# Two-layer decoder trunk on one core: another order of the first two groups of three FFNs, an earlier transpose in the last group, and lower bounds computed on all partitions

## The chip, the cores and the metric

The kernel runs on one core of a Trainium2 chip. The metric is device time in microseconds (us) of one execution. Engines are named as in the profile: PE (matrix multiply; PEld is its weight load), DVE (vector), ACT (scalar), POOL (GpSimd), SP (which issues nearly all DMAs).

## The reference

Two layers, each a half-step SwiGLU FFN, a token mixer and a second half-step FFN, with a layer norm after each. `x` is 256 x 1024, the FFN's inner width is 2816, all in float32.

```python
def swiglu(x, w_gate, w_up, w_down):
    return (jax.nn.silu(x @ w_gate) * (x @ w_up)) @ w_down

lb_all = jnp.cumsum(jax.nn.softmax(lb_param.astype(f32), axis=0), axis=0)
lb_all = lb_all - lb_all[0:1]
for l in range(DEPTH):                                            # DEPTH = 2
    x = layer_norm(ALPHA * x + 0.5 * swiglu(x, ffn1_gate[l], ffn1_up[l], ffn1_down[l]), ln_g[l, 0], ln_b[l, 0])
    h = x @ w_in[l]
    u = h[..., :D_POOL]
    q, f_raw, v, g = jnp.split(h[..., D_POOL:], 4, axis=-1)
    y_pool = multiscale_pool(u, pool_w[l], pool_scale[l])
    o = hgrn2_recurrence(q, f_raw, v, lb_all[l])                  # uses log(lb) and log1p(-lb)
    y_hgrn = head_rms_norm(o, hgrn_norm_g[l]) * jax.nn.silu(g)
    mix = jnp.concatenate([y_pool, y_hgrn], axis=-1) @ w_out[l]
    x = layer_norm(ALPHA * x + mix, ln_g[l, 1], ln_b[l, 1])
    x = layer_norm(ALPHA * x + 0.5 * swiglu(x, ffn2_gate[l], ffn2_up[l], ffn2_down[l]), ln_g[l, 2], ln_b[l, 2])
```

`lb_param` is 2 x 512. In layer 0 the lower bound is zero, so its logarithms (`la` and `lm`) are read only in the mixer of layer 1.

## The kernel before

There are four FFNs; in the order of time they are called FFN1 to FFN4 here. FFN1 and FFN3 are followed by a mixer each, FFN2 by FFN3. The 256 tokens are two halves `hf` of 128 partitions.

**Split products.** Each float32 product is three PE matmuls (`mm3`, L95 to L97): weight and activation are each split into a rounded part and a remainder. Every 512 KB weight tile arrives by an SP DMA in `raw` (a ring of 5 buffers); ACT makes the rounded part (`wh`, `xh` or `dh`, L101), and behind it DVE the remainder (`wl`, `xl`, `dl`, L102). So each weight costs a turn of ACT and a turn of DVE in the order in which these stand in the engines' queues. The finished parts lie in three rings: `w` (8), `x` (2) and `d` (6).

**An FFN** works in 11 groups of 256 inner columns. `G(g, hf)` multiplies half `hf` by gate and up weights of group g (24 matmuls of 512 columns); `gate` (L335) then takes silu on ACT (`sil`, L340) and multiplies on DVE (`hn`, L341). `T(g, hf)` (L401) transposes `hn` on PE (L404, two matmuls) into a PSUM tile named `gu`; ACT and DVE copy it out as `hth` and `htl` (L101, L102). `D(g, hf)` multiplies that by the down weights (12 matmuls into `acc`). For the groups 2 to 9 `GT(g)` (L307) does both halves at once, already transposed. `D(10, hf)` is followed by the layer norm of that half, whose inverse square root is POOL's (`rs`, L253), and later by transposes of the result (L185) for the next stage.

**What sets the order.** PE's instructions stand in the order in which the program issues them. `later(n, fn)` puts a piece of work behind n further `mm3`; `T` is such a piece, with 6 slots, or 4 for the first half of group 0 and the second half of group 10. If something needs its result first, `later.wait` issues it at once. The other engines' instructions are placed by the framework's scheduler, by priorities: `AHEAD` moves the gate's and `T`'s pieces up, `BEHIND` puts the weight loads back. Each engine then works strictly through its list.

**PSUM.** All of `G`, `T` and `GT` draw their `gu` tiles in turn from a ring of 4. `GT` takes four at once, and its first four matmuls write one each; the fourth is the tile of whatever drew last before `GT`. Before `GT(2)` that is `T(1,1)`, and its tile is free when its `htl` is done.

**The order in an FFN (L434 to L469).** FFN2 to FFN4 run G(0,0) G(1,0) D(0,0) G(0,1) D(1,0) G(1,1) D(0,1) GT(2) D(1,1), then GT(g), D(g-1,0), D(g-1,1) for g from 3, and at the end G(10,0) D(9,0) D(10,0) G(10,1) D(8,1) D(9,1) D(10,1). FFN1 has an opening of its own.

**`lower_bounds` (L473)** works out `la` and `lm` near the end of FFN1. It takes the two rows of `lb_param` spread over 128 partitions (two DMAs of 256 KB into a `raw` tile), and every one of its 128 x 512 operations repeats one and the same row in all partitions.

Of the kernel before, what the change touches and what calls it, by code (L numbers as in the profile page):

```python
# [10 lines left out]
F32 = mybir.dt.float32  # L11
F32R = mybir.dt.float32r
U8 = mybir.dt.uint8
AF = mybir.ActivationFunctionType
# [3 lines left out]
P = 128  # L18
D = 1024
S = 256  # L20
DEPTH = 2
# [3 lines left out]
NG = DFF // GW  # L25
NB = 5
NH = 4
# [47 lines left out]
def trunk(ctx: ExitStack, tc: tile.TileContext, t, out: bass.AP):  # L75
    nc = tc.nc
    pool = lambda name, bufs, **kw: ctx.enter_context(tc.tile_pool(name=name, bufs=bufs, **kw))
    cp = pool("const", 1)
    rawp = pool("raw", RAW)
    wp = pool("w", NW)  # L80
    xp = pool("x", 3)
    xtp = pool("xt", 1)
    sp = pool("small", 2)
    gbp = pool("gb", 1)
    psa = pool("psa", 4, space=PSUM)
    psg = pool("psg", 4, space=PSUM)
    ctx.enter_context(tc.manual_schedule(engines={mybir.EngineType.PE}))
    later = Later()
# [101 lines left out]
    def project(hf, ps, ws):  # L190

        xt = xT[hf]
        for kt in range(KT):
            later.wait(lambda: xt.done > kt)
            wh, wl = ws[kt // 2].parts
            cs = slice((kt % 2) * 512, (kt % 2) * 512 + 512)
            mm3(ps, xt.h[:, kt, :], xt.l[:, kt, :], wh[:, cs], wl[:, cs], kt == 0, kt == KT - 1)
            if kt % 2:
                ws[kt // 2].used()
# [13 lines left out]
    fix = cp.tile([P, 4, PAD], F32, name="fix")  # L213
    pscale = cp.tile([P, DEPTH, 4], F32, name="pscale")
    gn = cp.tile([P, DEPTH], F32, name="gn")
    la = cp.tile([P, 512], F32, name="la")
    lm = cp.tile([P, 512], F32, name="lm")

    def late_dma(dst, src):

        tc.keep_in_program_order(nc.sync.dma_start(dst, src))

    def load_consts():
        for j in range(2):
            cm = rawp.tile([P, 1024], F32, name="raw")
            late_dma(cm, t["cumM"][:, j, :])
            nc.scalar.copy(cumM[:, j, :], cm)
        st = rawp.tile([P, 896], F32, name="raw")
        late_dma(st, t["masks"])
        nc.vector.tensor_copy(masks, st)  # L230
        late_dma(fix, t["fix"].to_broadcast([P, 4, PAD]))
        late_dma(pscale, t["pscale"])
        late_dma(gn, t["gn"])

    def load_gb(l, i):
        g = gbp.tile([P, D], F32, name="lng")
        b = gbp.tile([P, D], F32, name="lnb")
        late_dma(g, t["ln_g"][l, i:i + 1, :].to_broadcast([P, D]))
        late_dma(b, t["ln_b"][l, i:i + 1, :].to_broadcast([P, D]))
        return g, b  # L240
# [25 lines left out]
    class FFN:  # L266
# [17 lines left out]
        def G(self, g, hf):  # L284
            ps = psg.tile([P, 2 * GW], F32, name="gu")
            project(hf, ps, self.gw[g])
            self.gate(g, hf, ps)
# [48 lines left out]
        def gate(self, g, hf, ps):  # L336
            sil = scope[0].tile([P, GW], F32, name="sil", bufs=2)
            hn = scope[0].tile([P, GW], F32, name="hn", bufs=2)
            with tc.high_priority(offset=AHEAD):
                nc.scalar.activation(sil, ps[:, 0:GW], AF.Silu)  # L340
                nc.vector.tensor_tensor(hn, sil, ps[:, GW:2 * GW], ALU.mult)  # L341
            later(4 if (g, hf) in ((0, 0), (NG - 1, 1)) else 6, lambda: self.T(g, hf, hn))

        def start(self):

# [65 lines left out]
        def D(self, g, hf):  # L411
            if self.turned(g):
                ht = [[p[:, place[hf], :] for p in self.ht[g, i]] for i in range(2)]
            else:
                later.wait(lambda: (g, hf) in self.ht)
                ht = [[p[:, i, :] for p in self.ht[g, hf]] for i in range(2)]
            if g == 0:
                self.accs[hf] = [psa.tile([P, 512], F32, name="acc") for _ in range(2)]
            if g == 4 and hf == 0:
                self.gb = load_gb(*self.ln)  # L420
                if self.first:
                    load_consts()
                    for n in range(2):
                        load_x(n)
            dw = [w.parts for w in self.dw[g]]
            for c in range(2):
                cs = slice(c * 512, c * 512 + 512)
                for i in range(2):
                    mm3(self.accs[hf][c], ht[i][0], ht[i][1], dw[i][0][:, cs], dw[i][1][:, cs],
                        g == 0 and i == 0, g == NG - 1 and i == 1)  # L430
            for w in self.dw[g]:
                w.used()
            if g == NG - 1:
                layer_norm(hf, self.accs[hf], 0.5 / ALPHA, self.gb, self.slots[hf], self.last)  # L434

        def run(self):
            G, GT, D = self.G, self.GT, self.D
            if self.first:
                self.start()
                D(0, 0)  # L440
                D(0, 1)
                GT(2)
                D(1, 0)
                D(1, 1)
            else:
                G(0, 0)
                G(1, 0)
                D(0, 0)
                G(0, 1)
                D(1, 0)  # L450
                G(1, 1)
                D(0, 1)
                GT(2)
                D(1, 1)
            for g in range(3, NG - 1):
                GT(g)
                D(g - 1, 0)
                if g < NG - 2:
                    D(g - 1, 1)
            G(NG - 1, 0)  # L460
            D(NG - 2, 0)
            D(NG - 1, 0)
            G(NG - 1, 1)
            if self.mixer_next:
                tc.keep_in_program_order(nc.scalar.preload_act_table_set("natural_log_exp_and_others"))
            if self.first:
                with tc.high_priority(offset=-BEHIND):
                    lower_bounds()
            for g in range(NG - 3, NG):  # L469
                D(g, 1)  # L470


    def lower_bounds():  # L473

        pr = rawp.tile([P, 2, 512], F32, name="raw")
        for i in range(2):
            late_dma(pr[:, i, :], t["lb"][i:i + 1, :].to_broadcast([P, 512]))
        p0, p1 = pr[:, 0, :], pr[:, 1, :]
        m, r = la, lm
        nc.vector.tensor_tensor(m, p0, p1, ALU.max)  # L480
        for p in (p0, p1):
            nc.vector.tensor_tensor(p, p, m, ALU.subtract)
            tc.keep_in_program_order(nc.scalar.activation(p, p, AF.Exp))
        nc.vector.tensor_tensor(m, p0, p1, ALU.add)
        for c in range(4):
            cs = slice(c * P, (c + 1) * P)
            nc.vector.reciprocal(r[:, cs], m[:, cs])
        for p in (p0, p1):
            nc.vector.tensor_tensor(p, p, r, ALU.mult)
        nc.vector.tensor_tensor(p1, p0, p1, ALU.add)  # L490
        nc.vector.tensor_tensor(p1, p1, p0, ALU.subtract)
        nc.vector.tensor_scalar(p0, p1, -1.0, 1.0, ALU.mult, ALU.add)
        for dst, v in ((m, p1), (r, p0)):
            nc.vector.tensor_scalar_max(dst, v, TINY)
            nc.scalar.activation(dst, dst, AF.Ln)
            nc.vector.tensor_scalar(v, v, 0.0, NEG, ALU.is_le, ALU.mult)
            nc.vector.tensor_tensor(dst, dst, v, ALU.add)

    def log_sigmoid(dst, src, tmp):
        nc.scalar.activation(tmp, src, AF.Abs)  # L500
# [326 lines left out]
def _layout(inputs):  # L827
    a = {k: np.asarray(v) for k, v in inputs.items()}

    def gu(gate, up):  # L830
        both = np.stack([gate, up], axis=2).reshape(DEPTH, KT // 2, 2, P, 2, NG, GW)
        return both.transpose(0, 5, 1, 3, 2, 4, 6).reshape(DEPTH, NG, KT // 2, P, ET)

    w_in = a["w_in"].reshape(DEPTH, KT // 2, 2, P, NB, 512)[:, :, :, :, [2, 1, 3, 4, 0]]
    cum, masks, fix = _constants()
    return {
        "x": a["x"].reshape(S, D),
        "xT": a["x"].reshape(S, KT, P).transpose(2, 1, 0),
        "gu": np.stack([gu(a["ffn1_gate"], a["ffn1_up"]), gu(a["ffn2_gate"], a["ffn2_up"])], axis=1),
        "dn": np.stack([a["ffn1_down"], a["ffn2_down"]], axis=1).reshape(DEPTH, 2, DFF // P, P, D),  # L840
        "win": w_in.transpose(0, 4, 1, 3, 2, 5).reshape(DEPTH, NB, KT // 2, P, ET),
        "wout": a["w_out"].reshape(DEPTH, KT, P, D),
        "pw": a["pool_w"].transpose(0, 2, 1, 3),
        "pscale": a["pool_scale"].reshape(DEPTH, 4, P).transpose(2, 0, 1),
        "lb": a["lb_param"],
        "gn": a["hgrn_norm_g"].T,
        "ln_g": a["ln_g"],
        "ln_b": a["ln_b"],
        "cumM": cum,
        "masks": masks,  # L850
        "fix": fix,
    }
# [17 lines left out]
```

## Time and profile before

| | |
|---|---|
| median of 3 runs | 976.71 us (975.88 to 979.17) |
| profiled execution, its own time | 976.44 us |
| its span, first to last instruction | 974.7 us |
| ACT busy, DVE busy | 520.1 us (53%), 661.6 us (68%) |
| POOL busy | 26.2 us (3%) |
| mean DMA rate | 185 GB/s, 55% of the 16 DMA engines' time |
| granted PE clock, mean | 0.995 |
| the four FFNs' first GT(2) begins at | 35.98 (FFN1), 330.08 (FFN2), 520.15 (FFN3), 811.90 us (FFN4) |

Times within the span are counted from its first instruction. A row of the timeline has the start, the duration, engine, line, operation, what it writes and reads, and in brackets the idle time of the engine before it with what ended that. Matmuls overlap: a 512-column one is shown with 0.39 us, but the next starts 0.23 us after it. Waits on PE are therefore measured here from start to start.

### The profile page before, as it was taken

How to read it: one execution, taken by the hardware profiler on the slowest of the kernel's cores; microseconds unless marked ns; L12 is line 12 of the kernel's file. 1: busy time of each engine (PE TensorE's matmuls, PEld its weight loads, DVE VectorE, ACT ScalarE, POOL GpSimd, SP SyncE). 2: the span in 40 equal slices, each digit the busy share in tenths (PEclk: the TensorE clock that was granted, in tenths of full speed). 3: DMA queues.
4: the chain of work that ended last, by engine and by line, in shares of the span. 5: the costliest groups of instructions: out<-in, count | busy, mean ns of one | idle time of the engine just before them, and what ended most of it. 6: DMA issues, size and time to landing. Idle time of an engine off the chain costs nothing.

```text
span 974.7 us, 13133 instructions
## 1 busy us (share of the span) xinstructions
PE 957.0 (98%) x4814; PEld 808.3 (83%) x4814; DVE 661.6 (68%) x1095; ACT 520.1 (53%) x810; POOL 26.2 (3%) x47
## 2 busy tenths in 40 slices
PE   9999999999999899999999999999999999999996
PEld 7888888788887788888887888888888887888885
DVE  6875655899689675656675665547897896665625
ACT  6766544376555655554346555433965466645420
POOL 0000000000010000000000000000001000000000
PEclk9999999999999999999999999999999999999998
DMA  7977865233427866565346666542334377766301
GB/s 283 340 260 249 275 230 174 97 124 124 164 87 236 304 192 225 197 208 173 106 165 237 226 220 213 174 151 97 124 136 154 109 277 260 228 214 209 127 1 44
DMA packets 51473, 180.67 MB, mean 185 GB/s; under 512 B 6096, under 2 KB 6352, under 8 KB 51408
## 3 DMA queue, kind: packets, MB, share of 16 engines
q1 hardware_dynamic: 51408, 179.83, 55.0%
q8 instruction: 38, 0.62, 0.3%
q14 instruction: 27, 0.22, 0.1%
HBM read 178.75 MB, written 1.05 MB: 184 GB/s over the span
## 4 chain that ended last, share of the span: by engine, by line
PE 62%; DVE 4%; DMA 3%; ACT 1%; issue 1%; DVEq 0%; SPq 0%; ACTq 0%
PE gu L307 27%; PE acc L95 6%; PE acc L97 6%; PE acc L96 6%; PE gu L97 4%; PE gu L95 4%; PE gu L96 4%; DMA raw<-in_gu 2%; DVE wl L102 2%; DMA raw<-in_dn 1%; PE acc L652 1%; DVE dl L102 1%; PE gu L185 1%; ACT wh L101 0%; PE acc L624 0%
## 5 line engine op out<-in xcount | busy, mean ns | idle before, releaser
L101 ACT CAST wh<-raw 128x1024 fp32r<-128x1024 f32 (+1 forms) x204 | 209.9, 1035 | 101.9 <-DMA raw<-in_gu 46.1
L102 DVE TENSOR_TENSOR wl<-raw,wh 128x1024 fp32r<-128x1024 f32 (+1 forms) x204 | 241.6, 1200 | 24.9 <-ACT wh L101 14.2
L307 PE MATMUL gu<-xt,wh 128*128 128x512 f32 x768 | 179.7, 390 | 0.0
L102 DVE TENSOR_TENSOR dl<-raw,dh 128x1024 fp32r<-128x1024 f32 x88 | 106.8, 1224 | 104.8 <-ACT dh L101 104.7
L307 PEld LDWEIGHTS gu<-xt,wh 128*128 128x128 f32 x768 | 144.4, 188 | 30.4
L101 ACT CAST dh<-raw 128x1024 fp32r<-128x1024 f32 x88 | 91.6, 1048 | 115.4 <-DMA raw<-in_dn 111.5
L95 PE MATMUL acc<-dh,hth 128*128 128x512 f32 x352 | 139.2, 395 | 1.8 <-ACT hth L101 1.8
L96 PE MATMUL acc<-dl,hth 128*128 128x512 f32 x352 | 137.7, 391 | 0.3 <-DVE dl L102 0.3
L97 PE MATMUL acc<-dh,htl 128*128 128x512 f32 x352 | 137.6, 391 | 0.0
L95 PE MATMUL gu<-wh,xt 128*128 128x512 f32 x336 | 135.2, 402 | 0.0
L97 PE MATMUL gu<-wh,xt 128*128 128x512 f32 x336 | 131.4, 391 | 0.0
L96 PE MATMUL gu<-wl,xt 128*128 128x512 f32 x336 | 131.0, 390 | 0.0
L307 PE MATMUL gu<-xt,wl 128*128 128x256 f32 x768 | 99.7, 283 | 0.0
L307 PEld LDWEIGHTS gu<-xt,wl 128*128 128x128 f32 x768 | 96.9, 191 | 2.0
L330 DVE TENSOR_TENSOR sil<-gu,sil 128x256 f32<-128x256 f32 x64 | 27.0, 422 | 86.1 <-ACT sil L329 86.1
L95 PEld LDWEIGHTS acc<-dh,hth 128*128 128x128 f32 x352 | 66.2, 188 | 14.8 <-ACT hth L101 2.8
L97 PEld LDWEIGHTS acc<-dh,htl 128*128 128x128 f32 x352 | 66.1, 188 | 14.4 <-DVE htl L102 0.6
L96 PEld LDWEIGHTS acc<-dl,hth 128*128 128x128 f32 x352 | 66.2, 188 | 13.2 <-DVE dl L102 1.1
L97 PEld LDWEIGHTS gu<-wh,xt 128*128 128x128 f32 x336 | 63.1, 188 | 13.5
L96 PEld LDWEIGHTS gu<-wl,xt 128*128 128x128 f32 x336 | 63.3, 188 | 12.2
L95 PEld LDWEIGHTS gu<-wh,xt 128*128 128x128 f32 x336 | 63.2, 188 | 12.1
L307 PE MATMUL gu<-xt,xh 128*128 128x512 f32 x256 | 64.9, 405 | 5.0 <-DVE htl L102 5.0
(156 smaller groups left out, 1039.4 us busy)
## 6 DMA issues: line engine op xcount, KB each, us to landing
raw<-in_gu SPq DMA_DIRECT2D x172, 512.0 KB, 4.4
raw<-in_dn SPq DMA_DIRECT2D x88, 512.0 KB, 4.5
raw<-in_win SPq DMA_DIRECT2D x40, 512.0 KB, 4.1
raw<-in_wout SPq DMA_DIRECT2D x16, 512.0 KB, 4.4
lng<-in_ln_g SPq DMA_DIRECT2D x6, 512.0 KB, 4.8
lnb<-in_ln_b SPq DMA_DIRECT2D x6, 512.0 KB, 5.9
raw<-in_gu SPq DMA_DIRECT2D x8, 256.0 KB, 5.8
raw<-in_cumM SPq DMA_DIRECT2D x2, 512.0 KB, 5.5
```

Source lines behind the costliest of these rows:

```text
L95: nc.tensor.matmul(ps, lh, wh, start=start, stop=False)
L96: nc.tensor.matmul(ps, lh, wl, start=False, stop=False)
L97: nc.tensor.matmul(ps, ll, wh, start=False, stop=stop)
L101: first = nc.scalar.copy(dst_h, src)
L102: return first, nc.vector.tensor_tensor(dst_l, src, dst_h.bitcast(F32), ALU.subtract)
L185: nc.tensor.transpose(pt[:, k - a, :], self.nat[:, k * P:(k + 1) * P], ident)
L307: nc.tensor.matmul(ps[i][part][:, 2 * S - w:], weight.parts[lo][:, c:c + P], x[:, 0:w], start=kt == 0 and not lo, stop=kt == KT - 1 and lo ...
L330: nc.vector.tensor_tensor(dst, p[:, 0:S], dst, ALU.add)
L652: nc.tensor.matmul(ps[B][0:rows, j, :], E[:, j, s0:s0 + rows], E[:, j, t0:t0 + ps[B].shape[2]], start=True, stop=True)
```

## The change

Three things are done.

1. In FFN2 to FFN4, `G(1, 1)` comes before `D(1, 0)`.
2. The slots of `T` change. T(10,0) gets 2 in place of 6, T(1,1) gets 4 in place of 6, T(0,0) gets 6 in place of 4; T(10,1) keeps 4. This holds for FFN1 too.
3. `lower_bounds` works on the 512 values as 128 partitions x 4 for each of the two rows (`pr` and `both`, 128 x 2 x 4), so it needs one small load (`lbs`, 4 KB, issued with the other constants) in place of two spread ones. Its two results are written to a DRAM tile `rows` by a DMA on POOL's queue, and two more DMAs on POOL's queue spread each row over the partitions of `la` and `lm`.

```diff
+    drp = pool("rows", 1, space=bass.MemoryType.DRAM)
+    lbs = cp.tile([P, 2, NH], F32, name="lbs")
...
         late_dma(gn, t["gn"])
+        late_dma(lbs, t["lb"])
...
-            later(4 if (g, hf) in ((0, 0), (NG - 1, 1)) else 6, lambda: self.T(g, hf, hn))
+
+            slots = {(NG - 1, 0): 2, (NG - 1, 1): 4, (1, 1): 4}
+            later(slots.get((g, hf), 6), lambda: self.T(g, hf, hn))
...
                 G(1, 0)
                 D(0, 0)
                 G(0, 1)
+                G(1, 1)
                 D(1, 0)
-                G(1, 1)
                 D(0, 1)
                 GT(2)
                 D(1, 1)
...
     def lower_bounds():
 
-        pr = rawp.tile([P, 2, 512], F32, name="raw")
-        for i in range(2):
-            late_dma(pr[:, i, :], t["lb"][i:i + 1, :].to_broadcast([P, 512]))
+        pr = sp.tile([P, 2, NH], F32, name="pr")
+        both = sp.tile([P, 2, NH], F32, name="both")
+        nc.vector.tensor_copy(pr, lbs)
         p0, p1 = pr[:, 0, :], pr[:, 1, :]
-        m, r = la, lm
+        m, r = both[:, 0, :], both[:, 1, :]
         nc.vector.tensor_tensor(m, p0, p1, ALU.max)
         for p in (p0, p1):
             nc.vector.tensor_tensor(p, p, m, ALU.subtract)
-            tc.keep_in_program_order(nc.scalar.activation(p, p, AF.Exp))
+        tc.keep_in_program_order(nc.scalar.activation(pr, pr, AF.Exp))
         nc.vector.tensor_tensor(m, p0, p1, ALU.add)
-        for c in range(4):
-            cs = slice(c * P, (c + 1) * P)
-            nc.vector.reciprocal(r[:, cs], m[:, cs])
+        nc.vector.reciprocal(r, m)
...
         for dst, v in ((m, p1), (r, p0)):
             nc.vector.tensor_scalar_max(dst, v, TINY)
-            nc.scalar.activation(dst, dst, AF.Ln)
             nc.vector.tensor_scalar(v, v, 0.0, NEG, ALU.is_le, ALU.mult)
+        nc.scalar.activation(both, both, AF.Ln)
+        for dst, v in ((m, p1), (r, p0)):
             nc.vector.tensor_tensor(dst, dst, v, ALU.add)
+        rows = drp.tile([2, P, NH], F32, name="rows")
+        nc.gpsimd.dma_start(rows.rearrange("i p c -> p i c"), both)
+        for i, dst in enumerate((la, lm)):
+            nc.gpsimd.dma_start(dst, rows[i:i + 1].rearrange("i p c -> i (p c)").to_broadcast([P, 512]))
...
-        "lb": a["lb_param"],
+        "lb": a["lb_param"].reshape(DEPTH, P, NH).transpose(1, 0, 2),
```

What the scheduler makes of it is seen in the engines' orders at three places. Line numbers of the changed kernel are 1 to 8 higher than those of before.

**DVE and ACT in FFN2, ahead of GT(2).** First DVE before. `hn_3207` is the gate of (1,1), `htl_3228` the copy of T(1,1); the `dl` are the two down weights of group 2, `wl_3190` and `wl_3202` the first weights of group 4.

```order
L102 TENSOR_TENSOR htl_3149<-gu_3145,hth_3148 128x256
L102 TENSOR_TENSOR wl_3166<-raw_3164,wh_3165 128x1024
L102 TENSOR_TENSOR dl_3172<-raw_3170,dh_3171 128x1024
L102 TENSOR_TENSOR dl_3178<-raw_3176,dh_3177 128x1024
L341 TENSOR_TENSOR hn_3207<-sil_3206,gu_3138 128x256
L102 TENSOR_TENSOR wl_3190<-raw_3188,wh_3189 128x1024
L102 TENSOR_TENSOR wl_3202<-raw_3200,wh_3201 128x1024
L102 TENSOR_TENSOR htl_3228<-gu_3224,hth_3227 128x256
```

DVE in the changed kernel, at the same place; `hn_3198` and `htl_3217` are those of (1,1), `wl_3181` and `wl_3193` the first weights of group 4.

```order
L103 TENSOR_TENSOR htl_3176<-gu_3172,hth_3175 128x256
L103 TENSOR_TENSOR wl_3150<-raw_3148,wh_3149 128x1024
L344 TENSOR_TENSOR hn_3198<-sil_3197,gu_3129 128x256
L103 TENSOR_TENSOR dl_3156<-raw_3154,dh_3155 128x1024
L103 TENSOR_TENSOR dl_3162<-raw_3160,dh_3161 128x1024
L103 TENSOR_TENSOR htl_3217<-gu_3213,hth_3216 128x256
L103 TENSOR_TENSOR wl_3181<-raw_3179,wh_3180 128x1024
L103 TENSOR_TENSOR wl_3193<-raw_3191,wh_3192 128x1024
```

The gate's `hn` has moved ahead of both `dl`, and the copy `htl` ahead of both `wl`. ACT before, at the same place:

```order
L101 CAST dh_3177<-raw_3176 128x1024
L340 ACTIVATE sil_3206<-gu_3138 128x256
L101 CAST wh_3189<-raw_3188 128x1024
L101 CAST wh_3201<-raw_3200 128x1024
L101 CAST hth_3227<-gu_3224 128x256
```

ACT in the changed kernel:

```order
L102 CAST wh_3149<-raw_3148 128x1024
L343 ACTIVATE sil_3197<-gu_3129 128x256
L102 CAST dh_3155<-raw_3154 128x1024
L102 CAST dh_3161<-raw_3160 128x1024
L102 CAST hth_3216<-gu_3213 128x256
L102 CAST wh_3180<-raw_3179 128x1024
L102 CAST wh_3192<-raw_3191 128x1024
```

The silu of (1,1) now stands ahead of both `dh`, and the copy `hth` ahead of both `wh` of group 4. FFN4 has the same two pieces.

**DVE in FFN3, ahead of GT(2),** in the changed kernel (`hn_4876` and `htl_4895` are those of (1,1); `wl_4816` and `wl_4828` belong to group 3, `wl_4859` and `wl_4871` to group 4):

```order
L103 TENSOR_TENSOR wl_4816<-raw_4814,wh_4815 128x1024
L103 TENSOR_TENSOR wl_4828<-raw_4826,wh_4827 128x1024
L103 TENSOR_TENSOR dl_4834<-raw_4832,dh_4833 128x1024
L103 TENSOR_TENSOR htl_4854<-gu_4850,hth_4853 128x256
L103 TENSOR_TENSOR dl_4840<-raw_4838,dh_4839 128x1024
L344 TENSOR_TENSOR hn_4876<-sil_4875,gu_4807 128x256
L103 TENSOR_TENSOR wl_4859<-raw_4857,wh_4858 128x1024
L103 TENSOR_TENSOR wl_4871<-raw_4869,wh_4870 128x1024
L103 TENSOR_TENSOR htl_4895<-gu_4891,hth_4894 128x256
```

Here the two `wl` of group 3 have come ahead of `dl`, but `htl` of (1,1) still stands behind both `wl` of group 4, as it did before.

**POOL at the end of FFN1.** Before, the two powers `rs` (the layer norm's halves 0 and 1) had only the mixer's clearing of `sum` tiles between them:

```order
L253 TENSOR_TENSOR rs<-rs,neghalf 128x1
L726 MEMSET sum_2607 128x4x16
L726 MEMSET sum_2608 128x4x16
L726 MEMSET sum_2609 128x3x16
L726 MEMSET sum_2610 128x2x16
L253 TENSOR_TENSOR rs<-rs,neghalf 128x1
```

In the changed kernel the three DMAs stand there too:

```order
L256 TENSOR_TENSOR rs<-rs,neghalf 128x1
L503 DMA rows<-both 128x2x4
L505 DMA la<-rows 128x512
L505 DMA lm<-rows 128x512
L734 MEMSET sum_2610 128x4x16
L734 MEMSET sum_2611 128x4x16
L734 MEMSET sum_2612 128x3x16
L734 MEMSET sum_2613 128x2x16
L256 TENSOR_TENSOR rs<-rs,neghalf 128x1
```

POOL's second `rs` now stands behind three DMAs, of which the second and third read what the first writes.

## The prediction

> **What bounds the kernel now.** I read the page first, then the waits of PE, then the timeline around each of them.
>
> ```profile
> PE 957.0 (98%) x4814; PEld 808.3 (83%) x4814; DVE 661.6 (68%) x1095; ACT 520.1 (53%) x810; POOL 26.2 (3%) x47
> ```
>
> PE is busy in 98% of the span, and the change removes no matmul. So the time can fall only by what PE waits, and by what it runs slowly after a wait. The waits by kind (us in total, times, longest):
>
> ```profile
> PE gu L307 <- DVE htl L102: 5.0, 3, 2.2
> PE acc L95 <- ACT hth L101: 1.8, 4, 0.5
> ```
>
> Three waits in GT for a copy `htl`, and four of a down product for a copy `hth`: FFN2 to FFN4 have one of the former each, all four FFNs one of the latter. These rows count the time after the modelled end of the matmul before. What PE loses I take from start to start, against 0.23 us for a 512-column matmul.
>
> The worst place is the start of GT(2) in FFN2:
>
> ```profile
> 328.95 0.39 PE L96 MATMUL acc<-dl,hth 128*128 128x512 f32 x1
> 329.18 0.39 PE L97 MATMUL acc<-dh,htl 128*128 128x512 f32 x1
> 329.89 0.44 PE L404 MATMUL gu<-ident,hn 128*128 128x128 f32 x2 [0.32 <-DVE hn L341]
> 330.08 0.95 PE L307 MATMUL gu<-xt,xh 128*128 128x512 f32 x3
> 333.22 0.97 PE L307 MATMUL gu<-xt,xh 128*128 128x512 f32 x3 [2.19 <-DVE htl L102]
> ```
>
> 328.95 to 329.18 shows the step of 0.23. T(1,1) comes 0.71 after the last matmul: 0.48 lost. Three matmuls of GT take 0.69 from 330.08, so the fourth could start at 330.77 and starts at 333.22: 2.45 lost. Behind it PE runs slowly:
>
> ```profile
> 333.00:337.00 4.00, 3.78 (x11) 3.02 (x12) 0.31 (x2) 1.99 (x2) 0.00 (x0) 0.67 0.77 303
> 334.02 4.05 PE L307 MATMUL gu<-xt,xh 128*128 128x512 f32 x10
> ```
>
> The first row is a stretch (busy time by engine, then the granted clock): 0.67 there, 1.00 elsewhere. Ten matmuls take 4.05 us, where 9 x 0.23 + 0.39 = 2.46 would do: 1.6 lost. So FFN2 loses 0.5 + 2.4 + 1.6 = 4.5 us here.
>
> By the Trainium skill, "TensorE: Matmul & The Clock Gate", Part 1: The HAM clock gate, PE's clock is halved after an idle window of about 3.4 us, in windows that run free of the kernel; the trace differs, since an idle time under 2.5 us was enough here. What that rule makes of the sum is under the rivals.
>
> FFN3 and FFN4 have the same stop without the slow clock:
>
> ```profile
> 520.15 0.94 PE L307 MATMUL gu<-xt,xh 128*128 128x512 f32 x3
> 522.48 0.51 PE L307 MATMUL gu<-xt,xh 128*128 128x512 f32 x1 [1.38 <-DVE htl L102]
> ```
>
> ```profile
> 811.23 0.39 PE L97 MATMUL acc<-dh,htl 128*128 128x512 f32 x1
> 811.71 0.44 PE L404 MATMUL gu<-ident,hn 128*128 128x128 f32 x2
> 811.90 0.94 PE L307 MATMUL gu<-xt,xh 128*128 128x512 f32 x3
> 814.31 0.50 PE L307 MATMUL gu<-xt,xh 128*128 128x512 f32 x1 [1.47 <-DVE htl L102]
> ```
>
> FFN3: 522.48 - 520.15 - 0.69 = 1.6. FFN4: 814.31 - 811.90 - 0.69 = 1.7, and T itself came 0.25 late: 2.0. The three starts together: **8.1 us**.
>
> **T(10,0) two slots behind its gate.** FFN1 and FFN3 as examples:
>
> ```profile
> 174.58 0.44 PE L404 MATMUL gu<-ident,hn 128*128 128x128 f32 x2 [0.16 <-DVE hn L341]
> 175.48 0.50 PE L95 MATMUL acc<-dh,hth 128*128 128x512 f32 x1 [0.46 <-ACT hth L101]
> ```
>
> ```profile
> 657.44 0.38 PE L404 MATMUL gu<-ident,hn 128*128 128x128 f32 x2
> 658.28 0.50 PE L95 MATMUL acc<-dh,hth 128*128 128x512 f32 x1 [0.46 <-ACT hth L101]
> ...
> 655.39 0.42 DVE L341 TENSOR_TENSOR hn<-sil,gu 128x256 f32<-128x256 f32 x1 [5.19 <-ACT sil L340]
> ```
>
> Six slots are never reached, since D(9,0) has four and D(10,0) then asks for T at once. From T to the next matmul pass 0.84 us, of which the two transposes need 0.14: 0.7 lost, with 0.1 for a slow second matmul 0.8. With 2 slots T stands six matmuls (1.4 us) earlier, at about 656.0 in FFN3. Its input `hn` is done at 655.81, so T does not wait, and six matmuls then cover the 0.84 us of the copy. I take 0.8 in FFN2, FFN3 and FFN4. In FFN1 `hn` was late as well:
>
> ```profile
> 172.18 0.69 DVE L480 TENSOR_TENSOR la<-raw 128x512 f32<-128x512 f32 x1 [5.16 <-DMA raw<-in_lb]
> 172.90 1.29 DVE L482 TENSOR_TENSOR raw<-raw,la 128x512 f32<-128x512 f32 x2
> 174.11 0.41 DVE L341 TENSOR_TENSOR hn<-sil,gu 128x256 f32<-128x256 f32 x1
> ```
>
> Three operations of the old lower bounds stood ahead of it, waiting for their DMA. In the order of the change these have gone far ahead, with 4 elements in place of 512; `hn` then ends at about 172.6 and T is due at 172.9. FFN1 saves 0.8 + 0.4 = 1.2. Together **3.6 us**, in bounds 0 and 3.6.
>
> **G(1,1) ahead of D(1,0), T(1,1) after 4 slots.** T(1,1) now stands between D(1,0) and D(0,1): D(0,1)'s twelve matmuls, 12 x 0.23 = 2.7 us, lie between it and GT(2). What this brings hangs on when `htl` can be done. DVE and ACT in FFN2 before:
>
> ```profile
> 325.24 1.23 DVE L102 TENSOR_TENSOR wl<-raw,wh 128x1024 fp32r<-128x1024 f32 x1
> 326.39 1.22 DVE L102 TENSOR_TENSOR dl<-raw,dh 128x1024 fp32r<-128x1024 f32 x1
> 328.28 1.23 DVE L102 TENSOR_TENSOR dl<-raw,dh 128x1024 fp32r<-128x1024 f32 x1 [0.67 <-ACT dh L101]
> 329.42 0.42 DVE L341 TENSOR_TENSOR hn<-sil,gu 128x256 f32<-128x256 f32 x1
> 330.35 2.49 DVE L102 TENSOR_TENSOR wl<-raw,wh 128x1024 fp32r<-128x1024 f32 x2 [0.51 <-ACT wh L101]
> 332.75 0.42 DVE L102 TENSOR_TENSOR htl<-gu,hth 128x256 fp32r<-128x256 f32 x1
> ```
>
> ```profile
> 327.19 1.05 ACT L101 CAST dh<-raw 128x1024 fp32r<-128x1024 f32 x1 [1.04 <-DMA raw<-in_dn]
> 328.15 0.38 ACT L340 ACTIVATE sil<-gu 128x256 f32<-128x256 f32 x1
> ```
>
> The silu stood behind `dh`, which waited for its DMA, and `htl` behind the two `wl`. In the new order silu and `hn` go ahead of both `dl`, and `htl` comes right behind these. The `dh` still waits for its DMA and ends at 328.24; the second `dl` then ends at 329.51, `htl` at 329.9. PE, without the 0.48 of lateness, would start its fourth matmul of GT(2) at 330.77 - 0.48 = 330.3. So `htl` is in time by 0.4 us. T(1,1) is due at 329.41 - 2.7 = 326.7; `hn`, behind the `wl` that ends at 326.47, is done at 326.9: 0.2 late, which the sum takes off. FFN2 saves 4.5 - 0.2 = 4.3, the slow clock with it. FFN4 has the same pieces of order: 2.0. In FFN3 `htl` stays behind both `wl`; those of group 3 now come earlier, and with them their `raw` buffers, but how much of this reaches `htl` no row says. The bounds are 0 and 1.6; I take 1.2, nearer the whole, since the lead of 2.7 is more than the 1.6 to be hidden. Together **7.5 us**.
>
> What PE does next is covered: GT(2) then reads weights of group 2, which DVE has finished before the rows above begin (their first `wl` is group 3's). G(1,1) uses the weights that G(1,0) had. T(0,0), now 6 slots behind its gate, has two `mm3` (1.4 us) left before D(0,0), against the 0.84 us of the copy; should ACT or DVE be full there, D(0,0) waits, which I bound by 0 and 1 us in each FFN and take at 0.
>
> **Lower bounds.** Some twenty DVE operations of 128 x 512 (0.69 us in the row at 172.18) become as many of 128 x 4. PE waited for none of them but `hn`, counted above, so the rest is worth 0. The two DMAs on SP give way to one small one. The three DMAs on POOL delay only POOL's second `rs`:
>
> ```profile
> L257 DVE SCALAR_TENSOR_TENSOR x<-x,rs,lnb x24: 742/746/753, 181.7 to 970.8; 128x512 f32<-128x512 f32 x24
> L252 DVE TENSOR_SCALAR rs<-mv x12: 146/153/155, 180.3 to 968.8; 128x1 f32<-128x1 f32 x12
> L253 POOL TENSOR_TENSOR rs<-rs,neghalf x12: 917/924/997, 180.6 to 969.1; 128x1 f32<-128x1 f32 x12
> ```
>
> ```profile
> 202.07 0.60 PE L185 MATMUL gu<-ident,x 128*128 128x128 f32 x4
> 188.01 0.42 DVE L102 TENSOR_TENSOR htl<-gu,hth 128x256 fp32r<-128x256 f32 x1
> raw<-in_lb SPq DMA_DIRECT2D x2, 256.0 KB, 4.1
> ```
>
> The new chain starts behind the `htl` that ends at 188.4: 13 small DVE operations at 0.15 (L252's) are 2.0 us, ACT's logarithm at most 0.4; `both` is ready by 190.9. PE wants the normalised half at 202.07, so `rs` must start by 202.07 - 0.75 - 0.92 - 0.2 = 200.2. That leaves POOL 9.3 us for one DMA to land (4.1 by the `in_lb` row, for far more bytes) and for issuing three; no row shows an issue on POOL, so 0 to 0.9 each, the length of its own power. 4.1 + 2.8 = 6.9: in time by 2.4, so 0.
>
> **The sum.** 3.6 + 7.5 = 11.1 us. The profiled execution took 976.44 us, 0.3 below the median of the runs; 976.44 - 11.1 = **965.3 us**, or 1.1% faster.
>
> **The rivals.**
>
> *DVE stays late.* The scheduler's order was made by its own times. Where a DMA lands later than in the rows above, `htl` still comes after PE; margins are 0.4 us in FFN2, unknown in FFN3. If half of the 8.1 us stays, the time is 976.44 - 3.6 - 4 = 968.8; if all of it, 972.8. For it speaks the queue of DMAs in that stretch (share 0.77 in the row at 333); against it that `htl` no longer waits behind group 4 in two of three FFNs. Chance 0.18.
>
> *The slow clock is not the stop's doing.* If the 3.4 us at low clock come anyway, 1.6 us return: 966.9. By the Trainium skill's rule named above, stops under 3.4 us cost no clock, which would be this case. Against it: it began right behind the longest stop, and nothing else in the trace shows it between start and end. Chance 0.05.
>
> *POOL holds the layer norm: slower.* If the three DMAs keep POOL beyond 200.2, PE stands at the transposes of 202.07. From 9.3 us on it costs PE as much as it is late; slower than before by 0.3% it is from 11.1 + 2.9 + 9.3 = 23.3 us on. At 8 us for each DMA (twice the `in_lb` row) POOL is free at 214.9: 14.7 late, with the slow clock 16.3, or 981.6 us. At 4.1 each it is 3.0 late, 968.3. Against it: only the first DMA must land before the others are issued. By the Trainium skill, "SBUF — State Buffer", SBUF: two separate sides, a DMA on POOL's queue can't write its descriptors while DVE runs a two-port operation, and one of 620 ns took 3100 so; three of that are 9.3 us, an estimate from that page, just at the limit. No run here shows such a DMA. Chance 0.06, of which 0.02 slower than before.
>
> *The change does nothing:* if other waits take all of it, 976. Chance 0.03.
>
> **How the numbers follow.** The forecast has 0.68, within 963 and 967. Low end: the sum with FFN3's whole 1.6 and T(1,1) not late is 11.7, and D(0,0) of FFN2, with the 1 us bounded above, could as well gain as lose it: 963.7, with some scatter 963. High end: to 970, which takes in half of the first rival, the clock, and POOL's 968.3. A measurement of this kernel tells 0.3% (2.9 us) from no change; so faster means under 973.5. Faster 0.93, same 0.05, slower 0.02.
>
> **What would show it.** In the changed profile: no GT wait for `htl` in PE's waits, or a small one in FFN3; no `acc` wait for `hth`; a granted clock of 1.00 between start and end; T(10,0) in the midst of D(9,0); POOL's second `rs` before 200; FFN1 shorter by 1.2. It would be wrong if PE waited at T(1,1) or T(10,0) instead, at D(0,0) for the later T(0,0), or at the transposes behind FFN1.

## The result, and the profile after

| | before | after |
|---|---|---|
| median | 976.71 us (5 runs, 974.63 to 979.17) | 968.14 us (5 runs, 967.02 to 968.72) |
| ratio to before, 95% interval | | 0.991 (0.989 to 0.993) |
| profiled execution, its span | 976.44, 974.7 us | 968.72, 967.0 us |
| granted PE clock, mean | 0.995 | 0.998 |

The change makes the kernel 0.9% faster: 8.6 us by the medians, 7.7 between the two profiled executions. The forecast was 11.1.

The page's line of busy time, after:

```profile
PE 956.0 (99%) x4814; PEld 806.9 (83%) x4814; DVE 653.5 (68%) x1093; ACT 520.0 (54%) x808; POOL 27.7 (3%) x50
```

PE has the same 4,814 matmuls. The waits of PE after (us in total, times, longest):

```profile
PE gu L381 <- DVE zero L378: 1.1, 1, 1.1
PE acc L96 <- ACT wh L102: 0.9, 1, 0.9
PE gu L186 <- DVE x L260: 0.7, 1, 0.7
PE gu L409 <- DVE hn L344: 0.2, 1, 0.2
PE acc L97 <- DVE dl L103: 0.2, 1, 0.2
```

Both rows of before have gone: no GT waits for `htl`, no down product for `hth`. Nothing of their size has come instead. PE in FFN2 around T(1,1) and GT(2):

```profile
326.81 0.39 PE L98 MATMUL acc<-dh,htl 128*128 128x512 f32 x1
327.04 0.38 PE L409 MATMUL gu<-ident,hn 128*128 128x128 f32 x2
327.17 0.48 PE L96 MATMUL acc<-dh,hth 128*128 128x512 f32 x1
...
330.02 3.90 PE L310 MATMUL gu<-xt,xh 128*128 128x512 f32 x16
```

T(1,1) starts 0.23 us after the matmul before it, and GT(2)'s first sixteen matmuls are one row of 3.90 us (15 x 0.23 + 0.39 = 3.84) where before three, a stop and thirteen at half clock stood. DVE at that place:

```profile
326.16 0.41 DVE L344 TENSOR_TENSOR hn<-sil,gu 128x256 f32<-128x256 f32 x1
326.80 2.54 DVE L103 TENSOR_TENSOR dl<-raw,dh 128x1024 fp32r<-128x1024 f32 x2 [0.23 <-ACT dh L102]
329.25 0.42 DVE L103 TENSOR_TENSOR htl<-gu,hth 128x256 fp32r<-128x256 f32 x1
```

`hn` is done at 326.57 for a transpose at 327.04, and `htl` at 329.67 for a fourth matmul at 330.02 + 0.69 = 330.71: in time by 1.0 us, where the prediction gave 0.4. GT(2) of FFN3 and FFN4 runs through as well:

```profile
516.26 3.90 PE L310 MATMUL gu<-xt,xh 128*128 128x512 f32 x16
```

```profile
806.11 3.90 PE L310 MATMUL gu<-xt,xh 128*128 128x512 f32 x16
```

T(10,0) now lies in the midst of D(9,0). In FFN1, on PE and then on DVE:

```profile
173.19 0.39 PE L98 MATMUL acc<-dh,htl 128*128 128x512 f32 x1
173.42 0.38 PE L409 MATMUL gu<-ident,hn 128*128 128x128 f32 x2
173.56 0.48 PE L96 MATMUL acc<-dh,hth 128*128 128x512 f32 x1
```

```profile
172.71 0.42 DVE L344 TENSOR_TENSOR hn<-sil,gu 128x256 f32<-128x256 f32 x1 [5.21 <-ACT sil L343]
```

Its `hn` is done at 173.13, ahead of 173.42; the three old operations of the lower bounds no longer stand in front of it. On POOL:

```profile
190.33 0.90 POOL L503 DMA_DIRECT2D rows<-both  x1 [9.43 <-ACT xt L102]
193.76 0.58 POOL L505 DMA_DIRECT2D la<-rows  x1 [2.52 <-DMA rows<-both]
194.33 0.54 POOL L505 DMA_DIRECT2D lm<-rows  x1
194.85 0.39 POOL L734 MEMSET sum<- 128x64 f32 x4
195.19 0.70 POOL L256 TENSOR_TENSOR rs<-rs,neghalf 128x1 f32<-128x1 f32 x1
```

The second `rs` starts at 195.19; the limit in the prediction was 200.2.

So everything that the change was forecast to do is there, and some 3 us are missing. I compared when each piece of work starts in the traces of before and after. The terms of the prediction read so (us won, each summed before it is rounded; T(10,0) from D(9,0)'s first matmul to G(10,1)'s first, a start from the FFN's first matmul to the 17th of GT(2)); the runs named at the right are explained below:

| | forecast | after | again | order_only | lbs_behind |
|---|---|---|---|---|---|
| T(10,0) in FFN1 | 1.2 | 1.1 | 1.1 | -0.2 | 1.1 |
| T(10,0) in FFN2 to FFN4 | 2.4 | 2.1 | 2.1 | 2.2 | 2.2 |
| start of FFN2 | 4.3 | 3.9 | 5.3 | 5.2 | 5.0 |
| start of FFN3 | 1.2 | 1.2 | 1.0 | 1.0 | 0.9 |
| start of FFN4 | 2.0 | 1.9 | 1.4 | 2.2 | 2.2 |
| sum of these | 11.1 | 10.1 | 10.8 | 10.6 | 11.4 |
| all the rest of the kernel | 0 | -2.3 | -1.4 | -0.1 | +0.4 |
| end of the last D(10,1) earlier by | 11.1 | 7.9 | 9.4 | 10.5 | 11.7 |

After, 2.3 us are lost in stretches where nothing was changed and nothing waits. They are lost in every block of matmuls, a little in each. The largest group of 512-column matmuls, that of `wh` in GT, before and then after (busy us in all, mean ns of one, idle time before):

```profile
L307 PE MATMUL gu<-xt,wh 128*128 128x512 f32 x768 | 179.7, 390 | 0.0
```

```profile
L310 PE MATMUL gu<-xt,wh 128*128 128x512 f32 x768 | 180.6, 391 | 0.0
```

The same 768 matmuls cost 0.9 us more. From start to start, over the some 3,190 pairs of 512-column matmuls that follow one another at 215 to 260 ns, the mean step is 228.2 ns before and 229.1 after: 3,190 x 0.9 ns = 2.9 us lost, of which the 256-column ones (119.4 to 119.1 ns) give back 0.3. Why the step of an unchanged matmul should grow became the question of the experiments.

### The profile page after: what moved, and what is told of

Same layout as the page of the kernel before. It is cut to its first block, busy times and chain, and to the rows that moved or that the text cites. A ratio compares the mean times of both kernels' runs of the same rounds, so it can differ in the third digit from the quotient of the medians.

```text
span 967.0 us, 13131 instructions
## 1 busy us (share of the span) xinstructions
PE 956.0 (99%) x4814; PEld 806.9 (83%) x4814; DVE 653.5 (68%) x1093; ACT 520.0 (54%) x808; POOL 27.7 (3%) x50
## 5 line engine op out<-in xcount | busy, mean ns | idle before, releaser
L310 PE MATMUL gu<-xt,xh 128*128 128x512 f32 x256 | 62.4, 396 | 0.0
```

The source lines that it names most:

```text
L310: nc.tensor.matmul(ps[i][part][:, 2 * S - w:], weight.parts[lo][:, c:c + P], x[:, 0:w], start=kt == 0 and not lo, stop=kt == KT - 1 and lo ...
```

## The experiments

Two theories of the loss. **Place**: `lbs` takes 32 bytes of every partition ahead of most tiles, so the tiles laid behind it lie 32 bytes further, and the matmul's step hangs on where tiles lie. As built, `wh` begins at byte 35,680 of a partition before and 35,712 after. The pool that an FFN opens for itself (`dh`, `dl`, `xh`, `xl`, `hth`, `htl`) is laid from the other end, by `side="right"` in the kernel, and does not move: `dh` begins at byte 147,424 in both. **Order**: matmuls that no longer stop meet more traffic of DVE, ACT or DMA, and are slowed by it. Beside these stood the question which part of the change brings what. Ratios below are to runs of the kernel before on the same chip, with 95% intervals; the mean step comes from each run's trace as above.

**The change once more.** No edit.

> The changed kernel once more, unaltered. In its first profile a 512-column matmul starts 229.3 ns after the one before it on average, before it 228.2 ns: over some 3,100 of them 3 us of the 3.4 us that the forecast missed. Theory A (the step belongs to the kernel, by where its tiles lie): the mean step is 229.3 ns again and the time 968. Theory B (the step scatters from execution to execution): another mean between 228 and 230 ns, and a profiled span that differs from 967.0 us by as much as the step says, 2.8 us per ns.

967.33 us (5 runs, 966.60 to 967.75), ratio 0.992 (0.991 to 0.993); step 229.2 ns. The loss repeats. The FFN2 opening scatters: in the first profile PE also stood 0.7 us at the transposes of L186, here not.

**The two parts apart.** order_only has the order and the slots with the old lower bounds:

```diff
+            slots = {(NG - 1, 0): 2, (NG - 1, 1): 4, (1, 1): 4}
+            later(slots.get((g, hf), 6), lambda: self.T(g, hf, hn))
...
+                G(1, 1)
                 D(1, 0)
-                G(1, 1)
```

> Order of the groups and slots of T as in the change, lower bounds as before. Theory A (the 32 bytes of the lbs tile shift all tiles behind it and lengthen the step): step 228.2 ns, time 965 to 966, faster than the whole change by 2 to 3 us. Theory B (scatter): 968 to 969, since only the 0.4 us of the late hn in FFN1 is lost. Both: no wait in GT(2) of FFN2 to FFN4, and T(10,0) of FFN1 late by 1.3 us, as hn stands behind the old operations, which wait for their DMA.

lb_only has the new lower bounds in the old order with the old slots: the changed kernel with the lines above as they were.

> Lower bounds as in the change alone, order and slots as before. Theory A: the step is 229.3 ns, and the time 2 to 3 us above before, 979. Theory B: 976 to 977, at most 0.4 us below before. Both: POOL's second power in FFN1 starts by 198 and PE does not wait at the transposes behind FFN1.

| | median us | ratio | step of 512 columns |
|---|---|---|---|
| again | 967.33 | 0.992 (0.991 to 0.993) | 229.2 ns |
| order_only | 966.14 (4 runs) | 0.991 (0.989 to 0.992) | 228.3 ns |
| lb_only | 978.04 (7 runs) | 1.002 (1.000 to 1.004) | 229.2 ns |

The longer step goes with the lower bounds, not with the order: order_only has the new order at the old step, lb_only the old order at the new step. That speaks against *order*. In FFN1, on the other hand, order_only shows what the new lower bounds are good for. Its DVE ahead of T(10,0):

```profile
172.52 1.29 DVE L484 TENSOR_TENSOR raw<-raw,la 128x512 f32<-128x512 f32 x2
173.73 0.41 DVE L341 TENSOR_TENSOR hn<-sil,gu 128x256 f32<-128x256 f32 x1
```

and the wait that follows:

```profile
PE gu L406 <- DVE hn L341: 1.4, 2, 1.1
```

`hn` ends 1.0 us later than after, T(10,0) waits 1.1, and FFN1 wins nothing by the 2 slots (-0.2 in the table). So the 1.1 won in FFN1 belong to both parts together.

lb_only's stop in FFN4 and the stretch behind it (the second fence: busy times by engine, granted clock, DMA):

```profile
810.66 0.94 PE L310 MATMUL gu<-xt,xh 128*128 128x512 f32 x3
814.35 4.84 PE L310 MATMUL gu<-xt,xh 128*128 128x512 f32 x13 [2.75 <-DVE htl L103]
```

```profile
815.00:819.00 4.00, 4.00 (x12) 3.12 (x11) 0.91 (x1) 1.99 (x2) 0.00 (x0) 0.57 0.62 234
```

The low clock stands in FFN4 here, behind a stop of 2.9 us (start to start, less a step), and not in FFN2, whose stop was 1.6 this time.

**The order without the slots.**

```diff
+                G(1, 1)
                 D(1, 0)
-                G(1, 1)
```

> G(1,1) ahead of D(1,0) alone, all slots as before: T(1,1) then stands two mm3 later, 1.4 us ahead of GT(2). If the group order carries the gain of the three starts, 976.7 - 7.6 = 969 and the four waits for hth remain (2.9 us). If the lead of T(1,1) over GT(2) is what counts, half of it brings about half: 972 to 973, with GT waits of about 1 us left in each of FFN2 to FFN4.

968.97 us (5 runs), ratio 0.994 (0.992 to 0.995). Its waits of PE:

```profile
PE acc L95 <- ACT hth L101: 1.9, 4, 0.5
...
PE gu L307 <- DVE htl L102: 0.2, 1, 0.2
```

The order alone takes nearly all of the `htl` waits (5.0 us before, 0.2 here) and the low clock; the four `hth` waits of the tails stay. That is 6.6 us of the 9.4 that order_only wins in the same runs. T(1,1), 6 slots behind its gate, still has six matmuls (1.4 us) between itself and GT(2), so half the lead of the change does nearly all, and not half.

**The slots without the order.**

```diff
-            later(4 if (g, hf) in ((0, 0), (NG - 1, 1)) else 6, lambda: self.T(g, hf, hn))
+            slots = {(NG - 1, 0): 2, (NG - 1, 1): 4, (1, 1): 4}
+            later(slots.get((g, hf), 6), lambda: self.T(g, hf, hn))
```

> The new slots of T alone, group order and lower bounds as before. T(10,0) gains 0.7 us in FFN2, FFN3 and FFN4 each and about nothing in FFN1, where hn stands behind the old lower bounds. T(1,1) with 4 slots lies where it lay, right ahead of GT(2), so the three waits for htl stay. Time 976 - 2.1 = 974, if the gain at the end of FFN2 is not lost later; 976 if it is.

973.37 us (12 runs, 970.61 to 975.89), ratio 0.998 (0.997 to 1.000), the interval just touching no change. Its waits:

```profile
PE gu L307 <- DVE htl L102: 5.5, 3, 2.2
...
PE gu L406 <- DVE hn L341: 1.2, 2, 0.9
```

All three `htl` waits are back. From D(9,0) to G(10,1) it wins 0.7, 0.7 and 0.8 in FFN2 to FFN4, as the change does. So the two pieces are nearly independent: the order is worth some 6.6 us, the slots the 2.2 of three tails (slots_only's own median is 1.6 below that of before).

**Which step of the new order does it: the gate's lead or the transpose's?** order_only with T(1,1) put off to 8 slots in FFN2 to FFN4. G(1,1), its silu and its `hn` stay early; T then stands directly ahead of GT(2).

```diff
-            slots = {(NG - 1, 0): 2, (NG - 1, 1): 4, (1, 1): 4}
+            slots = {(NG - 1, 0): 2, (NG - 1, 1): 4, (1, 1): 4 if self.first else 8}
```

> Group order and slots of the change, lower bounds as before, but T(1,1) of FFN2 to FFN4 with 8 slots in place of 4: its gate is as early as in the change, and T(1,1) stands right ahead of GT(2), as before it; on DVE its htl is then behind both wl of group 4 again. If the lead of T(1,1) and the place of htl in DVE's list carry the gain, GT(2) waits for htl by about 2 us in each of FFN2 to FFN4 again and the time is 972 to 974. If the earlier G(1,1) and its gate carry it, the waits are at most 0.5 us each and the time 967 to 968.

972.11 us (12 runs, 969.45 to 975.64), ratio 0.996 (0.995 to 0.998). DVE, and then PE, in FFN2:

```profile
325.33 0.41 DVE L341 TENSOR_TENSOR hn<-sil,gu 128x256 f32<-128x256 f32 x1
...
331.46 1.22 DVE L102 TENSOR_TENSOR wl<-raw,wh 128x1024 fp32r<-128x1024 f32 x1 [2.09 <-ACT wh L101]
332.60 0.42 DVE L102 TENSOR_TENSOR htl<-gu,hth 128x256 fp32r<-128x256 f32 x1
```

```profile
328.66 0.94 PE L307 MATMUL gu<-xt,xh 128*128 128x512 f32 x3
333.07 1.22 PE L307 MATMUL gu<-xt,xh 128*128 128x512 f32 x2 [3.48 <-DVE htl L102]
```

`hn` is done at 325.74, nearly three us ahead of its transpose, and PE stops all the same, 3.7 us long: T is issued late, so the scheduler puts `htl` behind both `wl` again, and the second `wl` waits 2.09 for its `wh`. From the opening to GT(2) the early gate alone wins 0.3 in FFN2 and nothing in FFN4. In FFN2 and FFN4 it is T's lead that brings `htl` ahead of `wl` and gives PE work meanwhile; which of these two counts for more was not taken apart. FFN3 kept its gain (1.2) without the lead: there the early gate is enough.

**The place alone.** The kernel before, with an unused tile of 32 bytes where `lbs` stands in the change:

```diff
     gn = cp.tile([P, DEPTH], F32, name="gn")
+    pad = cp.tile([P, 8], F32, name="pad")
+    nc.gpsimd.memset(pad, 0.0)
```

> The kernel before with one more constant tile of 32 bytes per partition that nothing reads, at the place where the change puts lbs (POOL clears it once at the start). If the place of the tiles sets the step between matmuls, the step rises from 228.2 to 229.2 ns and the time by 2 to 3 us, to 978 to 979. If the step comes with the new lower bounds (their DMAs, the DRAM tile, POOL's queue), it stays 228.2 ns and the time 976.

The changed kernel with a further pad of 32 bytes, so that its tiles lie 64 further than before, and one of 64 bytes (`[P, 16]`, 96 further; run once):

```diff
     lbs = cp.tile([P, 2, NH], F32, name="lbs")
+    pad = cp.tile([P, 8], F32, name="pad")
+    nc.gpsimd.memset(pad, 0.0)
```

> The changed kernel with 32 more bytes behind lbs, so that the tiles lie 64 bytes further than before. If only some places are slow and what matters is where a tile stands within 64 bytes, the step is 228.2 ns again and the time 967.5 - 3 = 964 to 965. If every further shift costs, or the new lower bounds are the cause, 229.2 ns and 967 to 968.

> The changed kernel with 64 more bytes behind lbs: 96 bytes further than before, 64 further than the change. By the place within 64 bytes it is as slow as the change: 229.2 ns, 967 to 968. If the place within 128 bytes counts it may differ from both.

And the changed kernel with `lbs` behind the large tiles, in the pool of the small ones, so that the tiles of weights and activations lie where they lay before:

```diff
-    lbs = cp.tile([P, 2, NH], F32, name="lbs")
+    lbs = sp.tile([P, 2, NH], F32, name="lbs")
```

> The changed kernel with lbs placed in the small pool, which lies behind the raw, weight and activation tiles: those lie where they lay before the change. If their place alone makes the longer step, the mean step is 228.2 to 228.3 ns and the time 967.5 - 3 = 964.5, with no wait in GT(2) and none for hth. If the new lower bounds had a part in it, the step is above 228.6 ns and the time 966 or more.

Sorted by how far the tiles are shifted (a long step is one of 232 ns or more; the rest have a mean of 227.1 to 227.4 ns in every kernel, the long ones 234.2 to 234.7):

| shift | kernel | median us | ratio | mean step | long steps |
|---|---|---|---|---|---|
| 0 | before | 975.01 to 976.71 | | 228.2 ns | 14.2% |
| 0 | reorder_only, slots_only, order_only, late_t11 | above | above | 228.2 to 228.3 | 14.3 to 14.9% |
| 0 | lbs_behind | 965.92 (6 runs) | 0.990 (0.989 to 0.992) | 228.3 | 15.0% |
| 32 bytes | after, again, lb_only | above | above | 229.1 to 229.2 | 24.0 to 24.7% |
| 32 bytes | before_pad32 | 976.78 (12 runs) | 1.002 (1.000 to 1.004) | 229.2 | 24.7% |
| 64 bytes | pad64 | 965.25 (6 runs) | 0.990 (0.988 to 0.993) | 228.5 | 19.1% |
| 96 bytes | pad96 | 965.28 (1 run) | | 228.6 | 19.7% |

The row of `wh` in before_pad32, and in lbs_behind:

```profile
L309 PE MATMUL gu<-xt,wh 128*128 128x512 f32 x768 | 180.7, 391 | 0.0
```

```profile
L310 PE MATMUL gu<-xt,wh 128*128 128x512 f32 x768 | 179.8, 390 | 0.0
```

An unused tile of 32 bytes in the old kernel makes the same step as the change, and moving `lbs` out of the way takes it back. All six traces without a shift and all four with one of 32 bytes fall apart cleanly. *Place* is shown, by the traces' steps: in the time, before_pad32 alone could not tell it, since 2 us are near its interval and the runs of before scatter by more. lbs_behind's time, too, falls between the two that were expected; its step does not. For 64 bytes 228.2 or 229.2 ns were expected, for 96 bytes 229.2 by the place within 64; neither came, and why they lie between stays open. Which tile's place matters was not tried, but it is not that of a matmul's own operands alone: none of those of `D` moves, and yet the share of long steps between two matmuls of `D` is 11 to 14% in the six traces without a shift and 22 to 25% in the four with 32 bytes.

lbs_behind and pad64 have the whole change without most of the loss, and beat the kernel before by 1.0%: 965.92 and 965.25, which can't be told from each other. again and they ran in different batches; by the ratios the gain over the change is about 0.15%, near what can be told, and by the steps 2.0 to 2.7 us (3,200 times 0.63 or 0.84 ns).

## Why the prediction was right, and where it was not

The forecast was 965.3, the measured median 968.14, inside the range of 963 to 970 and above the narrower range of the likeliest case.

*The starts of GT(2).* The mechanism holds, step by step. `hn` and `htl` stand ahead of what they stood behind, all three stops have gone, and with them the low clock. How much low clock there was to win is chance: the profiled execution of before had one such stretch (mean clock 0.995), and later runs of before have means from 0.992 to 0.999. 7.5 was forecast, 6.9 measured after, 6.9 to 8.5 in the four runs of the table. The lateness of 0.2 at T(1,1) in FFN2 did not come: `hn` was done 0.3 sooner than I had it (326.57 for 326.9) and T due 0.3 later (327.04 for 326.7). In FFN3 the order left `htl` behind both `wl`, and the 1.2 taken between bounds of 0 and 1.6 was 0.9 to 1.2. That it fits is in part luck: it was reasoned from the lead of 2.7, and late_t11 shows FFN3 gaining as much without that lead. D(0,0) of FFN2, which I had bounded by 1 us and taken at nothing, did no harm that repeats.

*What carries it.* The prediction named the lead of 2.7 us between T(1,1) and GT(2). For FFN2 and FFN4 late_t11 bears this out: without the lead the early gate brings 0.3 and 0.0, against 5.2 and 2.2 in order_only. The whole lead is not needed, since reorder_only has half of it and waits 0.2 in all. In FFN3 the early gate alone brings the 1.2.

*T(10,0).* 3.6 forecast, 3.2 measured. The three later FFNs give 0.7 each where I took 0.8. FFN1 gives 1.1 of 1.2, and order_only shows that it takes the new lower bounds for that, as the prediction had it. The 0.4 for a late `hn` does not repeat: reorder_only and before_pad32, with the old slots and the old lower bounds, have `hn` in time and are 0.4 shorter there.

*Lower bounds.* "The rest is worth 0" is the step that failed. The durations were right: the chain on DVE was done at 189.73 (190.9 forecast), POOL's second `rs` started 5 us ahead of its limit. But the tile `lbs` moved the tiles laid behind it by 32 bytes, and this made 10% more of 3,190 matmul steps 7 ns longer (2.2 us) and the others a little (0.7): 2.9 us, 0.3 of it given back by the narrower matmuls. The term was absent, since I counted instructions and waits, and not where the tiles lie. With it the account closes for after: 3.2 + 6.9 - 2.9 + 0.3 = 7.5 against 7.7 measured. For again it leaves 1.1 us open (10.8 - 2.9 + 0.3 = 8.2 against 9.3). For lbs_behind, where it is missing, the terms sum to 11.4 and its profiled execution took 964.88 against the 965.3 forecast.

*The rivals.* "DVE stays late" gave 968.8, close to what came, by a cause that the trace excludes: no GT waits for `htl`. A time near a rival's is no evidence for it. "The slow clock is not the stop's doing" fell: in the twelve profiled executions every stretch at low clock between start and end stands right behind a stop of GT(2), and the seven of them without such a stop have none. "POOL holds the layer norm" fell: the DMA from `both` landed in 3.1 us, and issuing the three cost POOL 0.90, 0.58 and 0.54. The trap of the Trainium skill, "SBUF — State Buffer", SBUF: two separate sides (3100 ns for a DMA on POOL's queue beside two-port DVE operations) did not show here: with DVE at work beside it, that DMA of 4 KB took no longer to land than the load of `lbs`, also 4 KB, on SP's queue (3.1 us). Whether DVE's operations there were of the two-port kind no run shows. "The change does nothing" fell with the result.

## What to carry to other kernels

A new constant tile, however small, shifts the tiles laid behind it, and where PE's time is matmuls back to back, that alone can cost as much as a wait (2.9 us here): put it behind the large tiles, or try two or three pads, and compare the start-to-start step of the same matmul in both traces before explaining a difference by waits. To take a wait from an in-order engine, issue the step that produces the operand (here the transpose) early enough that its copy is queued ahead of bulk work; bringing only its input forward left two of the three stops standing. A time that agrees with a theory proves little: the waits and the sum by stretches told the causes apart.

## What the hardware did that I had not expected

**The matmul's step hangs on the tiles' place.** Steps of 227 or of 234 ns, and a shift of 32 bytes raises the share of the long ones from 14-15% to 24-25%. Which matmuls are long hardly changes from one execution to the next: of the long steps of after, 98% are long at the same matmul in again, and of those of order_only 96% in lbs_behind; but of those of lbs_behind only 57% in after, where the tiles lie 32 bytes further.

Averaged over all steps, traffic beside them explains nothing: after, 29% of the steps at which DVE and ACT were both mostly idle are long, and 24% of those at which both were busy; 23% in the slices of the page that moved under 150 GB/s, 25% in those over 220. By the Trainium skill, "SBUF — State Buffer", SBUF: two separate sides, DMAs and engines can't get in one another's way there; the trace agrees, as far as those two shares go. Within the matmuls of `D`, though, 32% of the steps beside a busy ACT are long and 19% of those beside an idle one, so a part played by the other engines, whose `raw` and `wh` did move, is not excluded. What makes a step long stays open.

**The half clock comes behind stops from about 2 us on, not only of 3.4.** The fourteen stops of GT(2) in the five traces that have them, in us from start to start less one step:

```
low clock behind it:  2.03  2.12  2.36  2.39  2.91  3.24  3.65
full clock behind it: 1.38  1.43  1.50  1.55  1.60  1.64  2.09
```

The stop of 2.03 is that of before_pad32 in FFN4, with the stretch behind it:

```profile
817.67 4.75 PE L309 MATMUL gu<-xt,xh 128*128 128x512 f32 x13 [1.87 <-DVE htl L102]
```

```profile
819.00:823.00 4.00, 4.00 (x12) 3.13 (x11) 1.23 (x1) 2.49 (x3) 0.00 (x0) 0.57 0.53 190
```

The 2.09 is late_t11's in FFN4, whose thirteen matmuls then take 3.30 us. So by its length alone a stop of near 2 us can do either. It is settled by where the stop lies on a grid. In each of the five traces the changes of the granted clock lie whole multiples of 3.413 us apart: in before 324.27 us at full clock (95 of them), 3.41 at half, 631.47 at full (185). Cut along this grid, each of the seven stops ahead of a low clock has 1.98 to 3.20 us in a single interval, and the low clock begins with the next; none of the other seven has more than 1.64 in one. The 2.09 of late_t11 falls across a boundary as 1.28 and 0.81, the 2.03 of before_pad32 has 1.98 on one side. That fits the windows running free of the kernel, of which the Trainium skill speaks ("TensorE: Matmul & The Clock Gate", Part 1: The HAM clock gate), and not its idle time of about 3.4 us. Each such stretch lasts 3.4 us at half clock, so a stop of 2 us can cost 1.6 more.

**Kernels without these stops scatter less.** The kernels without them had 4 to 6 runs each within 1.2 to 3.0 us of each other; those with them, before among them, had 5 to 23 runs within 4.5 to 8 (of two sets of five, before's first lie within 4.5 and those of after within 1.7). The granted clocks go with this: 0.992 to 0.999 in the runs of before, 0.997 to 0.999 in the kernels without stops; one low stretch takes 0.5 x 3.41 / 975 = 0.0018 off the mean.
